# Reading expert sums later: a two-block network on one Trainium2 core, with a root table asked for elsewhere and thirty unread products at the start

## The chip, the core and the metric

The kernel runs on one core of a Trainium2 chip. The metric is device time in microseconds (us) of one execution; 2152.31 us is the median of three runs before the change. The engines that matter here are TensorE (PE; the loading of its stationary operand is PEld), VectorE (DVE), ScalarE (ACT) and the queue of SyncE (SP), which issues the transfers. GpSimd (POOL) does next to nothing.

## The reference, cut to what matters

A first block (adaptive norm, a mixer of three branches, a feed-forward layer) and two further layers run on 256 tokens of width 1024, all in float32. The last part is the mixture of experts, in which most of the bytes lie:

```python
cond = jax.nn.silu(c)
mod = (cond @ w_ada[l] + b_ada[l])[:, None, :]           # shift, scale and gate of the first norm
...
out = jnp.zeros_like(h)
for e in range(N_EXPERTS):                               # 8 experts, D 1024, inner width 3584
    out = out + gates[..., e:e+1] * ((jax.nn.silu(h @ wg[e]) * (h @ wu[e])) @ wd[e])
x = x + g2 * out
return rmsnorm(x, final_norm_w)                          # one last root for each token
```

## The kernel before, in words

**Products in three parts.** Each float32 weight is split into a high part (fp32r) and a low rest. `split` does it in two instructions on blocks of 128x1024: ACT copies the source to the high part (a CAST, L374), DVE subtracts that from the source for the low part (L339). `chunk` fetches a weight block of 1 MB (512x512) by one transfer into a raw buffer and splits it in two such splits; the raw buffer is free for the next transfer when both are through. `mm3` then makes three products of each pair (high by high, high by low, low by high). There are six pairs of split buffers in the expert stage.

**The expert stage.** The chosen tokens of an expert are gathered by products (`place`, `begin`, `gather`), go through seven blocks of 512 inner columns, and are added back by products (`scatter`). The four experts with most tokens are *large*, the others *small* (up to 64 tokens, whose high and low parts lie side by side in the stationary operand, so that two products do instead of three). Two chains of experts take turns, so that a step of a large expert is followed by one of a small one; such two steps are called a pair here. A step has 12 splits: four for `gate` (two chunks, `kh` 0 and 4), four for `up`, four for `down` of the step before (`prev`; two halves). Each product of 128x512 is one instruction on PE; a large step has 48 for gate and up and 24 for down, a small one 32 and 16.

**Who reads the sums.** ACT, DVE and PE work through their instructions in the order written. In `up`, the sum of gate is read by ACT straight behind gate's splits (L351, a Silu of 128x512, large; the small one's copy L2128 behind up's splits). `up_end`, behind the splits of down's first half, multiplies (DVE) or copies (ACT, L2138) the sum of up and turns the result by four transposes, or eight small products, on PE. `end`, in the next step behind gate's first chunk (`mids[0]`), copies the turned result as high part (ACT, L2160) and subtracts (DVE); down needs both. `mids` is a list of four places in the next step, behind each of its four chunks. `issue_after(i)` keeps an instruction behind `i` on its engine; beyond that a scheduler sets the order, and the order printed below is what it made.

**The start.** `ada_start` multiplies a column block of `w_ada` by `cond`: eight terms per block, of which DVE adds seven in `acc` (L343, L348) and PE takes the eighth (`wv(7)`) and the sum over `acc` as products with one column. `ada_end` adds the bias; only then can the norm be scaled, split and multiplied. `warm(n)` issues `n` products of 128x512 whose result nobody reads.

**The end.** Behind the last step comes a branch (`overflow`, not taken here, for an expert with more tokens than places), then the rest of `down`, the last `scatter`, the squares, the roots (L574, `rsqrt_s`) and the output. A function of ACT needs its table loaded (ACT_TABLE_LOAD); `self.dummy` receives a result that nobody reads, to have a table loaded early.

Of the kernel before, what the change touches and what calls it, by code (L numbers as in the profile page):

```python
# [8 lines left out]
F32 = mybir.dt.float32  # L9
# [203 lines left out]
class K:  # L213
# [440 lines left out]
    def ada_start(self, w, cond, p, cb):  # L654
        acc = self.take("ma")
        with self.scope():
            w0, w1 = self.raw(w, 0, 4, cb * 512, 512), self.raw(w, 512, 4, cb * 512, 512)
            wv = lambda k: w0[:, k] if k < 4 else w1[:, k - 4]
            self.ts(acc, wv(0), cond[:, 0:1])
            for k in range(1, 7):  # L660
                self.stt(acc, wv(k), cond[:, k : k + 1], acc, ALU.mult, ALU.add)
            for l, r in ((wv(7), cond[:, 7:8]), (acc, self.ones[:, :1])):
                for j in range(4):
                    self.last_mm = self.mm(p[:, cb * 4 + j : cb * 4 + j + 1], l[:, j * 128 : j * 128 + 128], r, cb < 2 and j == 0 and l is not acc, cb > 1 and j == 3 and l is acc, True)
        self.free(acc)
# [95 lines left out]
    def setup(self):  # L761
# [15 lines left out]
        nc.scalar.copy(self.one, self.ones[:, :1])  # L777
# [56 lines left out]
    def block1(self):  # L834
# [17 lines left out]
        with self.scope("d"):  # L852
# [12 lines left out]
            for half in range(2):  # L865
                with self.scope("s"):
                    p = self.psum()
                    self.ada_start(A["w_ada"][0], self.cond1, p, half)
                    if half:
                        product(1, 0)  # L870
                    self.ada_start(A["w_ada"][0], self.cond1, p, 2 + half)
# [1159 lines left out]
    def scatter(self, acc, PG, add, gain=None, part=(0, 1)):  # L2031
        with self.scope():
            for half in part:
                cs = slice(half * 512, half * 512 + 512)
                with self.scope():
# [4 lines left out]
                    else:  # L2040
                        y = self.med()
                        self.tt(y, acc[half], gain[:, cs], ALU.mult)
                        if half == 0:
                            self.act(self.dummy, y[:, :1], AF.Sqrt, bias=self.eps, scale=0.0)
# [9 lines left out]
    def moe(self, x, lg, rs):  # L2054
# [49 lines left out]

        def up(e, cb, mids):
            XH, XL = state[e][1][0], state[e][1][-1]
            g, ps = self.med(), []
            for nm in ("moe_w_gate_2", "moe_w_up_2"):
                p = self.take("pd")
                ps.append(p)  # L2110
                for kh in (0, 4):
                    with self.scope():
                        args = (W(nm, e), kh * 128, 4, cb * 512, 512)
                        c = self.chunk(*args)
# [9 lines left out]
                if not small[e] and nm == "moe_w_gate_2":  # L2124
                    self.act(g, p, AF.Silu)
            if small[e]:
                with self.tc.issue_after(self.last_hi.ins):
                    nc.scalar.copy(g, ps[0])  # L2128
            return g, p


        def up_end(e, g, pu):
            hu = self.take("r", 0)
            p = self.take("ps", 0)
            if small[e]:
                gu = self.med()
                with self.tc.issue_after(self.last_hi.ins):
                    nc.scalar.copy(gu, pu)  # L2138
                for i, a in enumerate((g, gu)):
                    for k in range(4):  # L2140
                        self.mm(p[:, i * 256 + k * 64 : i * 256 + k * 64 + 64], a[:, k * 128 : k * 128 + 128], self.cst("ident2"))

                def end():
                    with self.scope():
                        h = self.med()
                        self.act(h[:, :256], p[:, :256], AF.Silu)
                        self.tt(h[:, 256:], p[:, 256:], h[:, :256], ALU.mult)
                        v = hu[:, :512].rearrange("p (k h s) -> p k h s", k=4, h=2)
                        self.split(h[:, 256:].rearrange("p (k s) -> p k s", k=4), v[:, :, 0], v[:, :, 1])
                    self.free(p)  # L2150
                return hu, end
            with self.scope():
                h = self.med()
                self.tt(h, pu, g, ALU.mult)
                for k in range(4):
                    self.tr(p[:, k * 128 : k * 128 + 128], h[:, k * 128 : k * 128 + 128])

            def end():
                with self.tc.issue_after(self.last_hi.ins):
                    self.last_hi = nc.scalar.copy(hu[:, :512], p)  # L2160
                with self.tc.issue_after(self.last_lo.ins):
                    self.tt(hu[:, 512:], p, hu[:, :512].bitcast(F32), ALU.subtract)
                self.free(p)
            return hu, end

        def down(e, cb, hu, half):
            hh, hl = hu[:, :512], hu[:, 512:]
# [3 lines left out]
            with self.scope():  # L2171
                c = self.chunk(W("moe_w_down_2", e), cb * 512, 4, half * 512, 512)
                for k in range(4):
# [7 lines left out]
            if half:  # L2181
                self.free(hu)
# [19 lines left out]
        for e, cb in steps:  # L2202
            with self.scope():
                gp = up(e, cb, mids)
                mids = [[] for _ in range(4)]
                if cb == NB - 1:
                    self.free(*state[e][1])
                if prev:
                    down(*prev, 0)
                hu, end = up_end(e, *gp)  # L2210
                mids[0].append(end)
# [3 lines left out]
            prev = (e, cb, hu)  # L2215
# [25 lines left out]
        for half in range(2):  # L2241
            self.presplit(W("moe_w_down_2", NE - 1), (NB - 1) * 512, 4, half * 512, 512)
        self.q["pd"].append(self.q["ps"].popleft())
        self.overflow(x, gate, pos, scaled, ad, add, PP[0], cap)
        down(*prev, 0)
# [67 lines left out]
```

## Time and profile before

| | us |
|---|---|
| median of three runs | 2152.31 |
| the three runs | 2149.79, 2152.31, 2153.07 |
| the profiled execution | 2151.22 |
| its span, from first to last instruction | 2149.4 |

| engine | busy, share of the span |
|---|---|
| PE | 96% |
| DVE | 86% |
| ACT | 62% |
| PEld | 79% |

PE's share is an upper bound: its matmuls are pipelined and their ends modelled, so a matmul that waits behind its weights counts as busy. The waits for a semaphore are given by who waited and by which instruction ended the wait. Everything below is told in the profiled execution's own time (1.8 us of it lie outside the span), which is 1.1 us under the median.

### The profile page before, as it was taken

The page shows a single profiled execution, that of the slowest core. Times are in us where ns is not written, and L with a number is a line of the kernel's source. Part 1 is how long each engine was busy: PE and PEld are TensorE (multiplying, and loading weights), DVE is VectorE, ACT ScalarE, POOL GpSimd, SP SyncE. Part 2 cuts the span into 40 slices and gives each one's busy share as a digit, 9 for nine tenths or more (in the row PEclk, how much of TensorE's full clock was granted, in tenths as well). Part 3 has the DMA queues.
Part 4 walks back from the last instruction along what each step waited for, and adds up shares of the span by engine and source line. Part 5 has one row for each costly group of instructions (what it writes and reads, how often), then busy time and mean ns, then how long its engine had stood idle before and what let it go on. Part 6 is the DMA issues. An engine that isn't in the chain of part 4 may idle for free. (4 is left out here: it accounts for less than half of the span.)

```text
span 2149.4 us, 31135 instructions
## 1 busy us (share of the span) xinstructions
PE 2066.2 (96%) x11593; PEld 1706.1 (79%) x11593; DVE 1841.5 (86%) x2669; ACT 1325.3 (62%) x1857; POOL 2.1 (0%) x6
## 2 busy tenths in 40 slices
PE   6999999999999999999999999999999999999997
PEld 5987888889988878998997887777777777777765
DVE  6888985898888868888787999998998899998997
ACT  4544354454445435444765887777787778777775
POOL 0000000000000000000000000000000000000000
PEclk9999999999999999999999999999999999999997
DMA  7546767878843527885465899998999899998993
GB/s 306 192 165 214 264 219 255 298 296 303 302 160 117 150 100 262 310 342 212 139 253 188 329 400 368 356 387 321 391 343 377 348 365 377 355 383 322 386 371 140
DMA packets 99997, 610.70 MB, mean 284 GB/s; under 512 B 19156, under 2 KB 24061, under 8 KB 27773
## 3 DMA queue, kind: packets, MB, share of 16 engines
q1 hardware_dynamic: 99836, 608.64, 75.7%
q8 instruction: 92, 1.51, 0.3%
q14 instruction: 69, 0.56, 0.1%
HBM read 606.75 MB, written 3.42 MB: 284 GB/s over the span
## 5 line engine op out<-in xcount | busy, mean ns | idle before, releaser
L354 PE MATMUL pd<-k 128*128 128x512 f32 (+2 forms) x7408 | 1447.2, 349 | 37.8 <-DVE k L339 26.6
L339 DVE TENSOR_TENSOR k<-k,k 128x1024 fp32r<-128x1024 f32 (+2 forms) x1149 | 1229.8, 1112 | 184.4 <-ACT k L374 180.9
L354 PEld LDWEIGHTS pd<-k 128*128 128x128 f32 (+1 forms) x7408 | 1139.1, 190 | 269.3 <-DVE k L339 104.0
L374 ACT CAST k<-k 128x1024 fp32r<-128x1024 f32 (+2 forms) x1131 | 1039.6, 977 | 362.9 <-PE pd L354 184.6
L354 PE MATMUL ps<-k 128*128 128x512 f32 (+8 forms) x3031 | 576.2, 343 | 13.4 <-DVE k L339 3.8
L354 PEld LDWEIGHTS ps<-k 128*128 128x128 f32 (+4 forms) x3031 | 431.6, 179 | 112.1 <-DVE k L339 18.2
L348 DVE SCALAR_TENSOR_TENSOR k<-k,k 128x512 f32<-128x512 f32 (+1 forms) x257 | 188.3, 735 | 2.1 <-ACT k L351 0.2
L351 ACT ACTIVATE k<-pd 128x256 f32<-128x256 f32 (+1 forms) x125 | 57.2, 481 | 101.4 <-PE pd L354 98.5
L351 ACT ACTIVATE k<-k 128x256 f32<-128x256 f32 (+8 forms) x142 | 69.0, 500 | 79.3 <-DVE k L339 41.7
L339 DVE TENSOR_TENSOR k<-k 128x512 f32<-128x512 f32 (+13 forms) x277 | 93.6, 355 | 17.3 <-ACT k L351 12.4
L354 PEld LDWEIGHTS ps<-k,k 128*128 128x128 f32 x526 | 77.0, 199 | 12.4 <-DVE k L348 3.4
L339 DVE TENSOR_TENSOR k<-ps,k 128x512 fp32r<-128x512 f32 (+5 forms) x99 | 56.8, 579 | 24.8 <-PE ps L354 8.7
L354 PE MATMUL ps<-k,k 128*128 128x64 f32 (+3 forms) x526 | 75.0, 269 | 2.9 <-DVE k L348 2.9
L357 PE MATMUL ps<-k,k 128*128 128x128 f32 (+1 forms) x396 | 60.8, 278 | 16.7 <-DVE k L343 15.8
L357 PEld LDWEIGHTS ps<-k,k 128*128 128x128 f32 (+1 forms) x396 | 47.9, 143 | 30.5 <-DVE k L343 18.5
L339 DVE TENSOR_TENSOR k<-pd,k 128x512 f32<-128x512 f32 (+4 forms) x108 | 59.8, 568 | 12.5 <-PE pd L354 6.5
L351 ACT ACTIVATE k<-ps,k 128x128 f32<-128x128 f32 (+2 forms) x100 | 36.6, 446 | 42.8 <-DVE k L348 26.7
L348 DVE SCALAR_TENSOR_TENSOR k<-pd,k,k 128x255 f32<-128x255 f32 (+2 forms) x96 | 43.1, 474 | 4.4 <-ACT k L351 4.0
L2138 ACT COPY k<-pd 128x512 f32<-128x512 f32 x28 | 16.4, 586 | 48.2 <-PE pd L354 47.9
L345 DVE TENSOR_SCALAR k<-ps,k 128x128 f32<-128x128 f32 (+1 forms) x90 | 32.4, 405 | 10.5 <-PE ps L354 6.9
L348 DVE SCALAR_TENSOR_TENSOR k<-k 128x256 f32<-128x256 f32 (+7 forms) x121 | 36.9, 312 | 2.8 <-ACT k L351 1.1
L351 ACT ACTIVATE k<-ps 128x256 f32<-128x256 f32 (+2 forms) x30 | 12.4, 420 | 35.3 <-PE ps L354 35.3
(95 smaller groups left out, 416.1 us busy)
## 6 DMA issues: line engine op xcount, KB each, us to landing
k<-in_moe_w_up_dram SPq DMA_DIRECT2D x112, 1024.0 KB, 7.0
k<-in_moe_w_gate_dram SPq DMA_DIRECT2D x112, 1024.0 KB, 7.1
k<-in_moe_w_down_dram SPq DMA_DIRECT2D x112, 1024.0 KB, 7.2
k<-in_ada_w_dram SPq DMA_DIRECT2D x48, 1024.0 KB, 5.3
k<-in_w_in_dram SPq DMA_DIRECT2D x44, 1024.0 KB, 6.1
k<-in_w_ff_dram SPq DMA_DIRECT2D x32, 1024.0 KB, 6.0
k<-in_w_ada_dram SPq DMA_DIRECT2D x24, 1024.0 KB, 6.7
k<-in_cd_w_in_dram SPq DMA_DIRECT2D x14, 1024.0 KB, 4.9
```

Of the source, the lines that this page charges most:

```text
L339: return self.nc.vector.tensor_tensor(o, a, b, op=op)
L345: self.nc.vector.tensor_scalar(o, a, s1, s2, op0=op0, op1=op1)
L348: self.nc.vector.scalar_tensor_tensor(o, a, s, b, op0=op0, op1=op1)
L351: return self.nc.scalar.activation(o, a, f, **kw)
L354: return self.nc.tensor.matmul(o, l, r, start=start, stop=stop, skip_group_check=skip)
L357: return self.nc.tensor.transpose(o, i, self.ident[: i.shape[0], : i.shape[0]])
L374: self.last_hi = self.nc.scalar.copy(hi, src)
L2138: nc.scalar.copy(gu, pu)
```

## The change

Three edits. In the expert stage `up` no longer reads its sums: ACT's reading of gate (`gate_out`) comes behind the splits of down's first half, the reading of up (`up_out`) behind gate's first chunk of the next step, the turn behind the second chunk of the next step, and `end` behind the splits of down's first half of the next step, ahead of down's products. The sums and the turned result now take turns in three banks of `pd`. At the start, two terms of each of the first two column blocks go to PE instead of one, and 30 unread products are issued behind the instruction that makes their operand. At the end, the request for the last root's table moves from `scatter` (where it read a result of the experts) to a place behind the branch in the program, where it reads a constant.

```diff
-    def ada_start(self, w, cond, p, cb):
+    def ada_start(self, w, cond, p, cb, own):
...
-            for k in range(1, 7):
-                self.stt(acc, wv(k), cond[:, k : k + 1], acc, ALU.mult, ALU.add)
-            for l, r in ((wv(7), cond[:, 7:8]), (acc, self.ones[:, :1])):
+            for k in range(1, 8):
+                if k not in own:
+                    self.stt(acc, wv(k), cond[:, k : k + 1], acc, ALU.mult, ALU.add)
+            terms = [(wv(k), cond[:, k : k + 1]) for k in own] + [(acc, self.ones[:, :1])]
+            for i, (l, r) in enumerate(terms):
                 for j in range(4):
...
-        nc.scalar.copy(self.one, self.ones[:, :1])
+        one = nc.scalar.copy(self.one, self.ones[:, :1])
+
+        self.warm(30, one)
...
-                    self.ada_start(A["w_ada"][0], self.cond1, p, half)
+                    own = (7,) if half else (3, 7)
+                    self.ada_start(A["w_ada"][0], self.cond1, p, half, own)
...
                         self.tt(y, acc[half], gain[:, cs], ALU.mult)
-                        if half == 0:
-                            self.act(self.dummy, y[:, :1], AF.Sqrt, bias=self.eps, scale=0.0)
                         self.split(y, yh, yl)
...
-                if not small[e] and nm == "moe_w_gate_2":
-                    self.act(g, p, AF.Silu)
+            return ps
+
+        def gate_out(e, b):
+            b["g"] = self.take("ms", 0)
+            with self.tc.issue_after(self.last_hi.ins):
+                if small[e]:
+                    nc.scalar.copy(b["g"], b["ps"][0])
+                else:
+                    self.act(b["g"], b["ps"][0], AF.Silu)
+            self.free(b["ps"][0])
+
+        def up_out(e, b):
+            b["h"] = self.take("ms", 0)
             if small[e]:
                 with self.tc.issue_after(self.last_hi.ins):
-                    nc.scalar.copy(g, ps[0])
-            return g, p
+                    nc.scalar.copy(b["h"], b["ps"][1])
+            else:
+                with self.tc.issue_after(self.last_lo.ins):
+                    self.tt(b["h"], b["ps"][1], b["g"], ALU.mult)
+            self.free(b["ps"][1])
+
+        def turn(e, b):
+            p = b["p"] = self.take("pd", 0)
...
+        def end(e, b):
+            p, hu = b["p"], self.take("r", 0)
+            hi, lo = self.last_hi.ins, self.last_lo.ins
...
+                with self.tc.issue_after(hi):
                     self.last_hi = nc.scalar.copy(hu[:, :512], p)
-                with self.tc.issue_after(self.last_lo.ins):
+                with self.tc.issue_after(lo):
                     self.tt(hu[:, 512:], p, hu[:, :512].bitcast(F32), ALU.subtract)
...
-        def down(e, cb, hu, half):
+        def down(e, cb, b, half, after=()):
...
                 c = self.chunk(W("moe_w_down_2", e), cb * 512, 4, half * 512, 512)
+                for f in after:
+                    f()
+                hh, hl = b["hu"][:, :512], b["hu"][:, 512:]
...
-                gp = up(e, cb, mids)
...
-                if prev:
-                    down(*prev, 0)
-                hu, end = up_end(e, *gp)
-                mids[0].append(end)
+                b = {"ps": up(e, cb, mids)}
+            mids = [[] for _ in range(4)]
...
+            if prev:
+                down(*prev, 0, [lambda: end(prev[0], prev[2]), lambda: gate_out(e, b)])
+            else:
+                gate_out(e, b)
+            mids[0].append(lambda e=e, b=b: up_out(e, b))
+            mids[1].append(lambda e=e, b=b: turn(e, b))
...
         for half in range(2):
             self.presplit(W("moe_w_down_2", NE - 1), (NB - 1) * 512, 4, half * 512, 512)
+        end(prev[0], prev[2])
         self.q["pd"].append(self.q["ps"].popleft())
         self.overflow(x, gate, pos, scaled, ad, add, PP[0], cap)
+
+        self.act(self.dummy, self.eps, AF.Sqrt)
         down(*prev, 0)
```

ACT in the expert stage, before, from a small step's two readings to the next step's `end` of a large one (L2128 and L2138: gate and up of the small step; L351 of 128x256: its `end`; L351 of 128x512: gate of the large step; L2160: `end` of the large step; `k_63` and `k_64` are the two buffer areas, `pd` the sums):

```order
L2128 COPY k_63<-pd_68 128x512
L374 CAST k_64<-k_63 128x1024 x2
L2138 COPY k_63<-pd_69 128x512
L374 CAST k_64<-k_63 128x1024 x2
L351 ACTIVATE k_63<-pd_66 128x256
L374 CAST k_64<-k_63 128x1024 x2
L374 CAST k_64<-k_63 128x4x64
L374 CAST k_64<-k_63 128x1024 x4
L351 ACTIVATE k_63<-pd_67 128x512
L374 CAST k_64<-k_63 128x1024 x8
L2160 CAST k_64<-pd_66 128x512
```

The same stretch after (L2177: `end` of the large step; L2134 and L2144: gate and up of the small step):

```order
L2177 CAST k_64<-pd_68 128x512
L2134 COPY k_63<-pd_69 128x512
L374 CAST k_64<-k_63 128x1024 x4
L2144 COPY k_63<-pd_67 128x512
L374 CAST k_64<-k_63 128x1024 x8
L351 ACTIVATE k_63<-pd_69 128x256
L374 CAST k_64<-k_63 128x1024
L374 CAST k_64<-k_63 128x4x64
L351 ACTIVATE k_63<-pd_68 128x512
L374 CAST k_64<-k_63 128x1024 x11
```

The reading of a large gate moved from behind that gate's own four casts (the row x4) to behind the ten of gate, up and half of down; the reading of a small gate moved by two casts, that of a small up by four; `end` moved from behind the next gate's first two casts to behind ten.

PE in the expert stage, before: gate, up, first half of down, the turn of a large result (four transposes, L357), second half, gate and up of the next step:

```order
L354 MATMUL pd_67<-k_64 128x512 x24
L354 MATMUL pd_68<-k_64 128x512 x24
L354 MATMUL ps_70<-k_64 128x512 x8
L357 MATMUL ps_72<-k_65,k_63 128x128 x4
L354 MATMUL ps_71<-k_64 128x512 x8
L354 MATMUL pd_69<-k_64 128x512 x16
L354 MATMUL pd_67<-k_64 128x512 x13
```

After, from gate of a small step to up of the next large one (`pd_66` and `ps_72` are the large expert's two sums of down, `pd_68` x4 the turn of the large result, the rows of 128x64 that of the small one):

```order
L354 MATMUL pd_69<-k_64 128x512 x16
L357 MATMUL pd_68<-k_65,k_63 128x128 x4
L354 MATMUL pd_67<-k_64 128x512 x16
L354 MATMUL pd_66<-k_64 128x512 x2
L354 MATMUL pd_69<-k_65,k_63 128x64 x4
L354 MATMUL pd_66<-k_64 128x512 x10
L354 MATMUL ps_72<-k_64 128x512 x12
L354 MATMUL pd_68<-k_64 128x512 x24
L354 MATMUL pd_69<-k_65,k_63 128x64 x4
L354 MATMUL pd_67<-k_64 128x512 x24
```

The number of products is the same. The turn moved from between the halves of down to behind the next step's gate, and down now follows an `end` that stands two splits ahead of it.

ACT behind the branch, before (L351 of 128x1 is the request for the table, L351 x4 the squares, L574 the roots):

```order
L2260 UNCONDITIONAL_BRANCH x2
L351 ACT_TABLE_LOAD
L351 ACTIVATE k_65<-k_63,k_65 128x1
L374 CAST k_64<-k_63 128x512 x2
L351 ACTIVATE k_63,k_65<-k_63 128x512 x4
L574 ACTIVATE k_63<-k_63,k_65 128x1 x2
```

ACT behind the branch, after; and, as a piece of the difference, ACT far ahead of the expert stage, beside an older request of the same kind:

```order
L2285 UNCONDITIONAL_BRANCH x2
L374 CAST k_64<-k_63 128x512 x2
L351 ACTIVATE k_63,k_65<-k_63 128x512 x4
L574 ACT_TABLE_LOAD
L574 ACTIVATE k_63<-k_63,k_65 128x1 x2
```

```order
-L351 ACTIVATE k_65<-k_65 128x1
+L351 ACTIVATE k_65<-k_65 128x1 x2
```

The request, which now reads a constant alone, was moved by the scheduler out of the place where it is written to far ahead, where other tables are loaded behind it. The table of the roots is loaded behind the squares.

PE behind the branch, before (the first row is what is left of down) and after:

```order
L354 MATMUL ps_70<-k_64 128x512 x3
L354 MATMUL ps_71<-k_64 128x512
L354 MATMUL ps_73<-k_64 128x512
```

```order
L354 MATMUL ps_71<-k_64 128x512 x8
L354 MATMUL ps_70<-k_64 128x512 x8
L354 MATMUL ps_73<-k_64 128x512
L354 MATMUL pd_66<-k_64 128x512
```

All 16 products of the last down stand behind the branch now, before 3 did.

## Rows read from the trace of the kernel before

**Rows 1.** Windows by stage: us, busy time (and count) of each engine, clock, DMA.
```profile
0.00:60.00 60.00, 43.17 (x193) 36.36 (x194) 41.40 (x68) 26.91 (x45) 0.20 (x4) 0.97 0.77 300
60.00:1172.00 1112.00, 1089.21 (x7196) 957.71 (x7195) 922.77 (x1693) 544.98 (x891) 1.91 (x2) 0.99 0.63 226
1172.00:1254.40 82.40, 82.40 (x397) 68.91 (x396) 76.84 (x95) 69.02 (x81) 0.00 (x0) 1.00 0.86 320
1254.40:1284.10 29.70, 29.70 (x142) 24.64 (x142) 29.28 (x30) 23.97 (x29) 0.00 (x0) 1.00 1.00 408
1284.10:2046.90 762.80, 738.64 (x3334) 559.54 (x3333) 683.37 (x692) 590.05 (x723) 0.00 (x0) 1.00 0.94 363
2046.90:2130.60 83.70, 77.29 (x329) 55.73 (x327) 78.97 (x79) 64.48 (x78) 0.00 (x0) 0.96 0.76 293
2130.60:2149.40 18.80, 5.82 (x12) 3.15 (x11) 8.87 (x16) 5.91 (x14) 0.00 (x0) 0.55 0.16 58
```

**Rows 2.** Waits from 1284.1 to 2046.9: total us, times, longest us.
```profile
PEld pd L354 <- DVE k L339: 85.1, 181, 1.1
DVE k L339 <- ACT k L374: 66.7, 61, 6.7
ACT k L351 <- PE pd L354: 56.9, 28, 3.8
ACT k L2138 <- PE pd L354: 38.8, 20, 2.3
```

**Rows 3.** Waits of the transfer queue in the same stretch, the only row.
```profile
SPq L393 <- DVE k L339: 621.1, 263, 9.1
```

**Rows 4.** Groups by shape, same stretch: busy us, mean ns, idle before, releasers.
```profile
L339 DVE TENSOR_TENSOR k<-k,k 128x1024 fp32r<-128x1024 f32 x527 | 611.5, 1216 | 66.3 <-ACT k L374 66.0
...
L374 ACT CAST k<-k 128x1024 fp32r<-128x1024 f32 x527 | 516.0, 1052 | 0.9 <-PE pd L354 0.9
...
L351 ACT ACTIVATE k<-pd 128x512 f32<-128x512 f32 x23 | 13.8, 598 | 48.6 <-PE pd L354 48.6
```

**Rows 5.** Timeline inside two pairs: start, us, engine, instructions, idle before, releaser.
```profile
1606.10 0.59 ACT L2160 CAST k<-ps 128x512 fp32r<-128x512 f32 x1 [1.24 <-PE ps L357]
...
1609.62 0.68 DVE L339 TENSOR_TENSOR k<-ps,k 128x512 fp32r<-128x512 f32 x1
...
1618.41 0.59 ACT L2138 COPY k<-pd 128x512 f32<-128x512 f32 x1 [2.30 <-PE pd L354]
...
1622.22 3.01 PE L354 MATMUL ps<-k 128*128 128x512 f32 x12
...
1630.74 0.60 ACT L351 ACTIVATE k<-pd 128x512 f32<-128x512 f32 x1 [1.91 <-PE pd L354]
...
1632.30 4.63 DVE L339 TENSOR_TENSOR k<-k,k 128x1024 fp32r<-128x1024 f32 x4 [1.26 <-ACT k L374]
```

**Rows 6.** Timeline where one expert ends and the next is gathered.
```profile
1454.91 0.60 ACT L351 ACTIVATE k<-pd 128x512 f32<-128x512 f32 x1 [3.77 <-PE pd L354]
...
1460.08 5.23 DVE L339 TENSOR_TENSOR k<-k,k 128x1024 fp32r<-128x1024 f32 x5 [3.12 <-ACT k L374]
```

**Rows 7.** Timeline of the start, up to the first scaled norm.
```profile
12.62 1.11 PE L357 MATMUL ps<-k,k 128*128 128x128 f32 x4 [12.62 <-DVE k L343]
...
14.76 3.89 DVE L348 SCALAR_TENSOR_TENSOR k<-k,k 128x512 f32<-128x512 f32 x5
...
23.82 1.87 PE L354 MATMUL ps<-k,k 128*128 128x1 f32 x8 [1.55 <-DVE k L348]
...
25.56 4.50 PE L354 MATMUL ps<-k 128*128 128x512 f32 x10
```

**Rows 8.** Timeline behind the branch.
```profile
2134.11 1.62 PE L354 MATMUL ps<-k 128*128 128x512 f32 x3 [3.45 <-PEq L2260]
...
2134.86 1.28 ACT L351 ACT_TABLE_LOAD   x1 [6.17 <-DVE k L339]
...
2142.66 0.61 ACT L574 ACTIVATE k<-k,k 128x1 f32<-128x1 f32 x2
```

## What was predicted

> **What bounds the kernel now.** I read the busy time by stage first, then who waits for whom, then the timeline of single pairs. The stages before 1172 us are ordered by the change as before, but for the first 60 us; PE is busy for 1089 of 1112 us there [rows 1] and nothing in the diff reaches them. So the prediction is about three places: the expert stage (1172 to 2131 us), the first 30 us and the last 19 us.
>
> In the expert stage no engine is full. From 1284.1 to 2046.9 us lie 22 pairs of a large and a small step (23 readings of a large gate, one at each edge [rows 4]), 34.7 us each. DVE is busy for 683.4 of the 762.8 us, ACT for 590.1, the transfers for 0.94 of the time [rows 1]. DVE's idle 79.4 us end in 66.7 us on a cast of ACT [rows 2]. Is ACT too slow? Its cast takes 1052 ns against DVE's 1216 ns, and in front of its own casts ACT waits only 0.9 us in all [rows 4]. It is late because of what stands in its queue: 48.6 us before the 23 readings of a large gate [rows 4], 38.8 us before the copies of a small up, all ended by PE [rows 2]. One such place shows the mechanism: ACT stands still for 1.91 us until PE has finished gate, then needs 0.60 us to read it, and DVE has meanwhile run out of high parts for 1.26 us [rows 5]. ACT throws away the lead that it has over PE at every step, and PE then waits for DVE's low parts, 85.1 us in 181 small waits [rows 2]. No wait of ACT for a transfer is among the rows; the queue's transfers wait for DVE to free a raw buffer, 621 us [rows 3].
>
> That the three engines can go faster together is seen in one pair: from 1254.4 to 1284.1 us it took 29.7 us, with PE busy throughout, DVE for 29.28 us, and the transfers at 408 GB/s [rows 1].
>
> **Expert stage, the reading moved back.** The work is the same, instruction by instruction; only places change. A gate sum of a large step is now read behind ten casts of its step instead of four, the reading of up behind fourteen. There are six pairs of split buffers, so the cast that stands ahead of such a reading could not have started before PE had used the pair six splits earlier: by then the sum is finished, or nearly so. So ACT's waits for gate and up should go, and with them most of the 66.7 us of DVE.
>
> What is late next? DVE itself: 683.4 us of work. To this I add the 0.42 us that DVE was idle in the fast pair, 22 times: 9 us. The third part is the change of experts, six of them in the stretch, where ACT reads what the gather's products leave; that reading has no later place. At one of them DVE lacked a cast for 3.12 us, partly because ACT had waited 3.77 us for a gate sum [rows 6]. That part goes; I keep 4 us per change for the rest (gather, scatter), 24 us. 683.4 + 9 + 24 = 716 us, **46 us less** than 762.8. PE would allow it: 22 pairs at 29.7 us are 653 us, and at 0.25 us per product (12 in 3.01 us [rows 5]) the eight products of a scatter, and about as much again or a little more for a gather, make some 5 us per change, 685 us in all (an estimate). Bounds: if only the 48.6 us of large gates counted and a third of it reached DVE, 16 us; if DVE ran as in the fast pair and the changes cost nothing, 70 us.
>
> Before 1254 us PE is busy in every microsecond [rows 1], so nothing is won there. In the last small steps (2046.9 to 2130.6 us) DVE is busy for 78.97 of 83.7 us; I take 2 of the 4.7 idle us.
>
> **The new wait.** Down's products now need an `end` that is queued behind both splits of that half: two splits at 1.16 us (four in 4.63 us), a copy of 0.59 us, of which the subtraction of 0.68 us waits [rows 5]: 3.6 us at most from the moment when PE could have begun. Behind it on PE stand all of down, the next gate and the turn; DVE and ACT go on. It is covered where PE is behind DVE by more than that. A step with a large up and small down gives PE 64 products of 0.24 to 0.25 us and a turn, about 16.5 us, against 12 splits of DVE and the small `end`, about 14.7 us, so PE falls behind and arrives late. In the other kind of step PE has 56 products, about 14 us, against 15.2 us, and catches up by about 1.2 us less than it fell behind. So I cost the wait at nothing; it is the first rival below. The narrow turn behind two products of down needs ACT's copy of gate, queued straight behind `end`: 0.2 us at most, inside the wait for the subtraction.
>
> On SP the loads of the experts' numbers now stand together ahead of one transfer more. They wait for the ranking at about 1175 us, when the transfers are busy for 0.86 of the time [rows 1]; the stock of raw buffers hides a few us. Zero.
>
> **The start.** DVE saves one term in each of two blocks: 5 terms in 3.89 us, 0.78 us each, 1.56 us on the chain that ends with the four products of `acc` (recorded as eight) at 23.82 us, for which PE had waited [rows 7]. PE gains two groups of four products, each 1.87 us at the rate of that row, in gaps that were open before: from 14.9 to 23.8 us its other groups took about 5.3 us, so 3.7 more just about fit. The thirty products run while PE waits for its first work at 12.62 us [rows 7]. Ten such products took 4.50 us (0.45 us each, the lower of the clock's two levels, 1.2 GHz, though the column shows no drop there) [rows 7], 12 in 3.01 us at the upper [rows 5]; thirty from 2.2 us on end at about 15.7 us if all run at the lower level and at about 9.7 us at the upper one. If the clock is high when the groups run, each takes about half, and the chain ends up to 2.5 us earlier; if it is low, PE is the end of the chain and it is up to 2 us later. I take **1 us less**; PE is full after it, so it reaches the end.
>
> **The end.** The request for the table does not stay where it is written: the order puts it far ahead, and a load of 1.28 us now stands between the squares and the first root. So 1.28 us plus the request's 0.3 us leave the chain at 2134.86 us, and 1.28 us come back before 2142.66 us [rows 8]: 0.3 us won, not 1.6. Against that, 16 products stand behind the branch where 3 did; these took 1.62 us, 0.54 us each, at a clock of about half [rows 8]. They need only the last low part of `end`, so some run during the 3.45 us in which the engines go through the branch [rows 8]. 13 more at 0.45 to 0.54 us are 6 to 7 us; less the 3.45 us, about 3 us. The last `end` stands bare: one more hop between ACT and DVE, about 0.5 us. Together **3 us more** (bounds: 4 less if the clock holds, 6 more if nothing overlaps).
>
> **Sum.** 2151.2 - 46 - 2 - 1 + 3 = 2105 us, in the profiled execution's time, 1.1 us under the median shown.
>
> **The rivals.** (1) *PE runs dry at down.* If the 3.6 us wait is bare in every step, a pair costs 29.7 + 7.2 = 36.9 us instead of 34.7, 48 us more over 22 pairs: 2151 + 48 + 2, about 2200 us. It turns the sign once the bare part is over 2.5 us per step on average (half of 34.7 - 29.7). For it: the two splits and the copy are strictly ahead. Against: DVE and ACT keep working ahead during the wait, and PE's large step is longer than DVE's. Chance 0.08.
>
> (2) *The transfers are the bound.* At 716 us the stretch needs 363 x 762.8 / 716 = 387 GB/s, with the transfers already busy for 0.94 of the time. If 363 GB/s were what can be had over long stretches, DVE's idle time would only change its name: 2150 us. The fast pair ran at 408 GB/s, and no wait for a transfer shows, so chance 0.05. The Trainium skill has a rule to this effect (DMA: Bandwidth & Descriptors, "Where 436 GB/s comes from"): between HBM and on-chip memory some 358 GB/s per core bind, and by it the stage would gain nothing. The trace disagrees: 363 GB/s over 763 us and 408 GB/s in a pair are above it; the same page's measured 425 GB/s for one core alone fits better.
>
> (3) *The waits come back.* DVE runs ahead and then waits for split buffers that PE holds, or the changes of experts spread their stall over the neighbouring pairs. The idle time before PE's weights is 85.1 us in many small waits [rows 2], some of which are DVE's own pace. A third of the gain would stay: 2151 - 16 + 2, about 2136 us. Chance 0.15.
>
> **How the numbers follow.** Forecast 0.72, (3) 0.15, (1) 0.08, (2) 0.05. The forecast's own range is 2078 to 2126 us (70 us won to 25 us won in the stage, with the ends of start and end). With most of (3) the range is 2078 to 2140 us; left out are (1), (2), a part of (3) and a corner below. Faster by over 0.2% (4.3 us, about what can be told from no change): 0.72 + 0.15 = 0.87; the same 0.05; slower 0.08.
>
> **What the profile after would show.** Right: readings of gate and up with hardly any idle time before them; DVE's wait for casts from 66.7 us to under 30; pairs of 30 to 33 us; transfers near 390 GB/s; a table load ahead of the first root. Wrong: PE waiting for ACT's copy of `end` before down by 2 us or more per step (1); ACT waiting for transfers (2); ACT or DVE waiting for PE's release of split buffers, with pairs still over 33.5 us (3).

## The result

| | us |
|---|---|
| kernel before, median on the same chip | 2151.05 |
| changed kernel, median | 2118.32 (2117.22 to 2124.44) |
| ratio, with 95% interval | 0.9854 [0.9832, 0.9876] |
| profiled execution of the changed kernel, and its span | 2124.44, 2121.5 |

The change wins 32.7 us, where 46 were forecast. The profiled execution is the slowest of the four. Part of that lies where the change does nothing: the exponential of the router, the last step ahead of the experts, began at 1164.6 us here, and between 1157.6 and 1164.6 us in all nine kernels that have the changed start. So I compare stretches, not spans, and measure the expert stage from that exponential to the end of DVE's last low part ahead of the branch ("the stage"), and the rest from there ("the end"). The stage repeats well from kernel to kernel: 969.3 and 969.0 us in the two kernels with the old expert part, 934.3 to 935.4 us in the six with the new one.

| us | before | changed | difference |
|---|---|---|---|
| up to the router's exponential | 1161.3 | 1164.6 | +3.3 |
| the stage | 969.25 | 935.37 | -33.9 |
| in it: 22 pairs between 23 readings of a large gate | 762.8 | 730.2 | -32.6 |
| the end | 18.86 | 21.58 | +2.7 |

### The profile page after: what moved, and what is told of

It is laid out like the page before. It is cut to its first block, busy times and chain, and to the rows that moved or that the text cites. A ratio compares the mean times of both kernels' runs of the same rounds, so it can differ in the third digit from the quotient of the medians.

```text
span 2121.5 us, 31382 instructions
## 1 busy us (share of the span) xinstructions
PE 2043.6 (96%) x11639; PEld 1740.5 (82%) x11639; DVE 1841.2 (87%) x2667; ACT 1336.6 (63%) x1857; POOL 2.1 (0%) x6
## 5 line engine op out<-in xcount | busy, mean ns | idle before, releaser
L354 PE MATMUL pd<-k 128*128 128x512 f32 (+2 forms) x7414 | 1416.4, 347 | 23.3 <-DVE k L339 14.3
L354 PE MATMUL ps<-k 128*128 128x512 f32 (+5 forms) x3055 | 573.2, 345 | 28.6 <-DVE k L339 17.5
L354 PEld LDWEIGHTS ps<-k 128*128 128x128 f32 (+2 forms) x3055 | 449.0, 182 | 125.2 <-DVE k L339 27.6
L351 ACT ACTIVATE k<-k 128x256 f32<-128x256 f32 (+9 forms) x143 | 69.2, 498 | 79.5 <-DVE k L339 42.2
L351 ACT ACTIVATE k<-pd 128x256 f32<-128x256 f32 (+1 forms) x148 | 65.7, 463 | 47.4 <-PE pd L354 44.6
L354 PE MATMUL pd<-k,k 128*128 128x64 f32 (+1 forms) x472 | 69.8, 288 | 5.8 <-ACT k L2134 5.1
L354 PEld LDWEIGHTS pd<-k,k 128*128 128x128 f32 x472 | 63.6, 193 | 12.1 <-ACT k L2134 6.2
L351 ACT ACTIVATE k<-ps,k 128x128 f32<-128x128 f32 (+2 forms) x100 | 37.3, 447 | 34.2 <-DVE k L348 27.1
L357 PE MATMUL ps<-k,k 128*128 128x128 f32 x302 | 47.2, 281 | 5.2 <-DVE k L343 4.3
L339 DVE TENSOR_TENSOR k<-ps,k 128x512 f32<-128x512 f32 (+5 forms) x52 | 30.8, 605 | 23.1 <-PE ps L354 15.0
L357 PEld LDWEIGHTS ps<-k,k 128*128 128x128 f32 x302 | 36.7, 145 | 15.5 <-DVE k L343 7.1
L345 DVE TENSOR_SCALAR k<-ps,k 128x128 f32<-128x128 f32 (+1 forms) x90 | 32.7, 405 | 12.2 <-PE ps L354 8.8
L357 PE MATMUL pd<-k,k 128*128 128x128 f32 (+1 forms) x222 | 36.8, 281 | 4.0 <-DVE k L1351 4.0
L357 PEld LDWEIGHTS pd<-k,k 128*128 128x128 f32 (+1 forms) x222 | 28.1, 143 | 10.9 <-DVE k L1351 4.4
```

The costliest lines, as they stand in the source:

```text
L339: return self.nc.vector.tensor_tensor(o, a, b, op=op)
L345: self.nc.vector.tensor_scalar(o, a, s1, s2, op0=op0, op1=op1)
L351: return self.nc.scalar.activation(o, a, f, **kw)
L354: return self.nc.tensor.matmul(o, l, r, start=start, stop=stop, skip_group_check=skip)
L357: return self.nc.tensor.transpose(o, i, self.ident[: i.shape[0], : i.shape[0]])
```

## The profile after

Windows of the changed kernel, columns as in [rows 1]: the first full pair and the 22 pairs behind it.

```profile
1260.20:1290.38 30.18, 30.18 (x144) 25.24 (x143) 29.94 (x31) 26.55 (x32) 0.00 (x0) 1.00 1.01 410
1290.38:2020.58 730.20, 704.68 (x3332) 576.97 (x3331) 684.52 (x694) 600.68 (x725) 0.00 (x0) 0.99 0.97 380
```

DVE's work in the 22 pairs is what it was, 684.5 us; its idle time fell from 79.4 to 45.7 us. ACT's groups by shape in that stretch:

```profile
L374 ACT CAST k<-k 128x1024 fp32r<-128x1024 f32 x528 | 526.6, 1051 | 66.6 <-PE pd L354 46.4 <-PE ps L354 14.5 <-issue 2.6
L351 ACT ACTIVATE k<-pd 128x512 f32<-128x512 f32 x23 | 13.6, 591 | 0.0
L2144 ACT COPY k<-pd 128x512 f32<-128x512 f32 x22 | 12.9, 588 | 0.0
L2134 ACT COPY k<-pd 128x512 f32<-128x512 f32 x22 | 12.9, 585 | 0.0
```

No reading of gate or up is waited for any more (48.6 us before the large gates alone [rows 4]); DVE's 22 multiplications of a large up have no idle time before them either. ACT now stands ahead of its casts instead, 66.6 us where it was 0.9 [rows 4]: it is as far ahead as the six pairs of split buffers let it, and PE's release of a buffer ends the wait. The waits of the same stretch (total us, times, longest us) say who still suffers:

```profile
ACT k L374 <- PE pd L354: 48.5, 110, 2.1
DVE k L339 <- ACT k L374: 33.4, 47, 4.5
...
PE ps L354 <- DVE k L339: 16.1, 16, 2.4
ACT k L2003 <- PE ps L357: 14.0, 5, 5.8
```

DVE's wait for casts fell from 66.7 [rows 2] to 33.4 us. Where its largest pieces lie, the timeline shows. L2003 is the copy by which `place` reads its turned slots; PE is still in the products of a large step when ACT comes to it.

```profile
1518.99 3.25 PE L354 MATMUL pd<-k 128*128 128x512 f32 x13
...
1522.49 0.38 ACT L2003 CAST k<-pd 128x256 fp32r<-128x256 f32 x1 [5.77 <-PE pd L357]
...
1523.85 2.36 DVE L339 TENSOR_TENSOR k<-k,k 128x1024 fp32r<-128x1024 f32 x2 [4.53 <-ACT k L374]
```

This is the mechanism that the change removes, at a place which the change leaves as it was: ACT waits 5.77 us in front of a sum that PE reaches late, and DVE is out of casts for 4.53 us. ACT waits for 1.0 to 5.8 us at the other five such copies, too (the row of 14.0 us), and behind all six DVE is out of casts for 13.6 us together.

## The experiments

**One edit at a time.** The expert edit alone on the kernel before, and the start alone.

```diff
 # the expert edit alone: the changed kernel with
-        self.warm(30, one)
-                    own = (7,) if half else (3, 7)      # ada_start as before
-        self.act(self.dummy, self.eps, AF.Sqrt)         # the request back in scatter
```

> The edit of the expert stage alone on the kernel before; start and request for the table as before. My terms of the prediction, corrected by the trace after: 23 pairs of 33.06 instead of 34.45 us give 32 us, the last steps and the bare end cost about 2, so 2151 - 30 = 2121 us; a pair 33.1 us. By the prediction as written (start 1 us won, the request at the end 0.3 us won): the whole change's 2118 us plus 1, 2119 us. If the start after costs 1 us, as its trace suggests, this kernel is 1 us faster than the whole change: 2117 us. In the trace: the first product behind the start's norm at 49.4 us as before.

0.9842 [0.9829, 0.9855]; the stage 934.3 us, the end 17.6 us. The whole gain is the expert edit's, and alone it has an end that is 4 us shorter than in company.

```diff
 # the start alone: the kernel before with
+        self.warm(30, one)
+                    own = (7,) if half else (3, 7)
```

> The start alone on the kernel before (thirty products and the terms given to PE). Prediction: 1 us won, 2150 us; the products behind the start's norm begin a microsecond earlier than 49.35 us. Rival, from the trace after: PE's clock has fallen when the groups of one-column products run, PE is now the end of that chain, and the clock falls once more at 38 us: 1 us lost, 2152 us, the product at 50.3 us. Second rival: the microsecond in the trace after was a later arrival of the transfers (0.55 us at the first term), and nothing is won or lost.

0.9996 [0.9987, 1.0005], nothing that the time can tell. The product behind the norm came at 49.34 us as before (49.35), but PE's first work on data had come 0.75 us later (13.37 for 12.62 [rows 7]). From there to the ten unread products it is 12.16 us instead of 12.94, and to the product behind the norm 35.97 instead of 36.73, so 0.8 us are won on the chain. The second rival (arrival) holds for the rest: PE's first work came as late, at 13.28 and 13.22 us, in two kernels with the start of before.

**The thirty products.** The changed kernel without them.

```diff
-        self.warm(30, one)
```

> The changed kernel without its thirty unread products; two terms per block still go to PE. Theory A (the thirty products make the clock fall at 14 us, and PE's way through the branch longer): the clock holds while the one-column products run, the ten unread products come 11 us after PE's first work instead of 12.15, and the end takes 19 us as with the start of before. Theory B (the terms do it): clock 0.5 from 15 us on, 12.2 us, and 21.5 us at the end. The time is 0 to 3 us under that of the whole change.

0.9851 [0.9836, 0.9866], as the whole change. At the start theory A falls: 12.15 us with and without the thirty. The changed kernel: its last group of one-column products in the timeline, then the window from 14 to 28 us (the clock is the third figure from the end).

```profile
18.48 6.98 PE L354 MATMUL ps<-k,k 128*128 128x1 f32 x32 [0.41 <-DVE k L348]
```

```profile
14.00:28.00 14.00, 12.75 (x56) 12.07 (x56) 10.00 (x19) 2.03 (x5) 0.00 (x0) 0.52 1.02 424
```

The same two views of the kernel without the thirty:

```profile
18.08 6.99 PE L354 MATMUL ps<-k,k 128*128 128x1 f32 x32 [0.23 <-DVE k L348]
24.93 4.61 PE L354 MATMUL ps<-k 128*128 128x512 f32 x10
```

```profile
14.00:28.00 14.00, 13.77 (x58) 13.10 (x59) 9.83 (x18) 2.43 (x6) 0.00 (x0) 1.00 1.01 423
```

The clock's column differs (0.52 and 1.00), the 32 products take 6.98 and 6.99 us. The 0.8 us come from DVE's saved terms. The thirty products buy nothing: behind them eight one-column products took 0.95 us at 13.67 us, but behind a gap of PE of 0.84 us the next eight, at 16.37 us, took 1.71 us, as without the thirty (1.71 us at 16.14). At the end the number is A's, 19.0 us; whether the thirty are its cause is taken up below.

**The end.** The request back in the scatter, the start as before, and the request behind the first cast of the last scatter.

```diff
 # request as before                                     # start as before: see the first diff
+                        if half == 0:
+                            self.act(self.dummy, y[:, :1], AF.Sqrt, bias=self.eps, scale=0.0)
-        self.act(self.dummy, self.eps, AF.Sqrt)
```

> The changed kernel with the request for the roots' table back in the scatter, as before. The kernel with the expert edit alone ended 17.6 us after DVE's last instruction before the branch, the changed one 21.6 us after it; this run and the next tell which of the two other edits costs these 4 us. Theory A, the moved request does: 17.6 us here and about 4 us less time than the whole change (2113 us). Theory B, the start does (its 38 more instructions on PE stand ahead of the branch): 21 us or more here, the time as that of the whole change or 0.3 us above. Theory C, it is chance of one execution: anything from 17 to 22 us here and in the next.

> The changed kernel with the start as before. Theory A (the moved request costs the 4 us at the end): 21.6 us from DVE's last instruction before the branch to the end, the time as that of the whole change. Theory B (the start does): 17 to 18 us, some 4 us less time. At the start itself: the ten unread products 12.94 us after PE's first work instead of 12.15.

```diff
 # request behind the first cast, in scatter
                         self.split(y, yh, yl)
+                        if half == 0:
+                            with self.tc.issue_after(self.last_hi.ins):
+                                self.act(self.dummy, self.eps, AF.Sqrt)
...
-        self.act(self.dummy, self.eps, AF.Sqrt)
```

> The changed kernel, with the request for the roots' table put behind the first cast of the last scatter. Theory: in the changed kernel the load of 1.28 us lies bare between the squares and the first root; here it lies between two casts that wait for PE anyway: the stretch from DVE's last instruction before the branch to the end from 21.6 to 20.3 us, the time 1.3 us less than the whole change (2117 us). Rival: the load only pushes the second cast, whose sum DVE reads at once, and nothing is won: 21.6 us.

0.9843 [0.9829, 0.9856], 0.9839 [0.9825, 0.9852] and 0.985 [0.9836, 0.9863]: in time none differs from the whole change. The traces do:

| start | request | PE idle in the branch, us | the products behind it | the end, us |
|---|---|---|---|---|
| as before | as before (expert edit alone) | 2.61 | 16 in 3.96 | 17.6 |
| as before | moved | 2.61 | 16 in 3.94 | 19.1 |
| changed | as before | 4.27 | 16 in 5.53 | 19.6 |
| changed | moved (the change) | 4.13 | 17 in 6.70 | 21.6 |
| changed | behind the first cast | 4.09 | 16 in 5.96 | 20.8 |
| no thirty | moved | 2.60 | 16 in 3.92 | 19.0 |

In these rows, one execution each, the moved request costs 1.5 us (first two) or 1.9 us (next two). The expert edit alone, behind the branch (DVE, ACT):

```profile
2094.78 3.96 PE L354 MATMUL ps<-k 128*128 128x512 f32 x16 [2.61 <-DVE k L339]
2097.99 0.69 DVE L339 TENSOR_TENSOR k<-ps,k 128x512 f32<-128x512 f32 x1 [3.26 <-DVEq L2282]
2098.76 1.28 ACT L351 ACT_TABLE_LOAD   x1 [4.49 <-DVE k L339]
2098.84 0.69 DVE L339 TENSOR_TENSOR k<-ps,k 128x512 f32<-128x512 f32 x1 [0.15 <-PE ps L354]
```

and the one with the start as before and the request moved:

```profile
2099.21 3.94 PE L354 MATMUL ps<-k 128*128 128x512 f32 x16 [2.61 <-DVE k L339]
...
2102.69 0.69 DVE L339 TENSOR_TENSOR k<-ps,k 128x512 f32<-128x512 f32 x1 [3.54 <-DVEq L2281]
2104.12 0.69 DVE L339 TENSOR_TENSOR k<-k,k 128x512 fp32r<-128x512 f32 x1 [0.74 <-ACT k L374]
2104.73 0.68 DVE L339 TENSOR_TENSOR k<-ps,k 128x512 f32<-128x512 f32 x1
...
2110.24 1.28 ACT L574 ACT_TABLE_LOAD   x1
```

With the request in scatter, DVE reads both sums of down one behind the other, the second while ACT loads the table (2097.99, 2098.84). Without it, DVE's low part of the first half stands ahead of the reading of the second (2102.69, 2104.12, 2104.73), and the load comes bare at the end. So the load and request of before were not simply 1.6 us on the chain: DVE's second reading ran beside them. That is read from these rows; no run changes the order of the two readings alone. Behind the first cast the request won 0.8 of the 1.3 us expected, with one more load of 1.28 us ahead of that cast.

The other 2.1 to 2.5 us go with PE's longer way through the branch and the low clock that follows (6.70 us for 17 products at a granted clock of 0.59, instead of 3.96 for 16 at 1.00). The thirty products go with the long way in all six rows, but a kernel below that has them took 2.61 us, and one without them ran its 17 products in 7.24 us, at 0.57, behind 2.62 us. What decides both is left open. Nor is theory C, chance of one execution, out: four kernels below with the start and the request of the change end in 19.3 to 21.4 us.

**What is left at the changes of experts.** `place`'s copy read two chunks later, in the next step:

```diff
-            p = self.psum()
+            p = self.take("ps", 0) if later is not None else self.psum()
...
-            self.nc.scalar.copy(PG, p[:, :256])
+            def read():
+                with self.tc.issue_after(self.last_hi.ins) if later is not None else nullcontext():
+                    self.nc.scalar.copy(PG, p[:, :256])
...
+            read() if later is None else later.append(read)
...
+            mids[0] += later
+            later.clear()
```

> The changed kernel, with ACT's copy of place's turned slots (L2003) read two chunks of casts later, in the next step. Theory A (what is left at the changes of experts is ACT standing before that copy; DVE lacks casts behind its six places for 1.1 to 4.6 us, 13.6 us in all): 10 to 13 us less than the whole change, 2106 us, and the pairs with a place 1 to 4.5 us shorter. Theory B (those pairs are full for PE, whose products of gather and scatter come on top, and DVE's idle time there is slack): only PE's own idle behind it comes back, 1.3 us at two places: 2115 to 2118 us, while L2003 no longer waits.

0.9841 [0.9828, 0.9855]; 2115.0 us in all, which is still within B; the stage took 929.9 us instead of 935.4, between the theories: 5 us of 13. L2003 no longer waits, but the wait has moved to ACT's readings of gather's sums (L351), and DVE starves there. Waits in its 22 pairs, then two rows of its timeline:

```profile
DVE k L339 <- ACT k L374: 31.7, 37, 3.9
...
ACT k L351 <- PE ps L354: 21.2, 5, 5.0
```

```profile
1668.94 0.70 ACT L351 ACTIVATE k<-ps,k 128x64 f32<-128x64 f32 x2 [4.99 <-PE ps L354]
...
1670.61 2.36 DVE L339 TENSOR_TENSOR k<-k,k 128x1024 fp32r<-128x1024 f32 x2 [3.94 <-ACT k L374]
```

So gather's sums were read one chunk later as well, on the same scheme:

```diff
-            return [lambda k0=k0: self.gather(x, P, ad["a2"], ad["b2"], out, (k0,)) for k0 in (0, 4)]
+            go = lambda k0: self.gather(x, P, ad["a2"], ad["b2"], out, (k0,), later)
+            return [lambda: go(0), lambda: (later.pop(0)(), go(4)), lambda: later.pop(0)()]
...
-                return [lambda: self.gather_small(x, P, ad["a2"], ad["b2"], X)]
+                return [lambda: self.gather_small(x, P, ad["a2"], ad["b2"], X, later), lambda: later.pop(0)()]
```

> As the kernel with place's copy read later, and the sums of gather are read one chunk later too. In that kernel the wait had moved: its pairs of 42.3 and 35.9 us hold ACT's readings of gather's sums, which wait for PE for up to 5.0 us (21.2 us in all), and DVE lacks casts for 3.6 to 3.9 us behind them. Theory A (ACT standing before sums at the changes of experts is what is left): DVE's wait for casts from 31 to under 15 us, 8 to 12 us less time than that kernel, 2104 us. Theory B (PE and DVE are full there in turn): the wait goes on to the next place, at most 3 us less.

0.9755 [0.9742, 0.9769], 2098.2 us: **20 us less than the change**, and the fastest of all. The stage took 915.9 us. Its 22 pairs and its waits:

```profile
1283.46:1994.29 710.83, 695.24 (x3331) 574.70 (x3330) 682.51 (x694) 603.88 (x725) 0.00 (x0) 1.00 0.97 390
```

```profile
DVE k L339 <- ACT k L374: 17.3, 39, 2.1
```

Theory A in sign, and more than it in size: 16.7 us less than the kernel before it (14.0 in the stage) where 8 to 12 were named, though DVE's wait for casts fell to 17.3 us and not to under 15. PE is busy for 695.2 of the 710.8 us (an upper bound), DVE for 682.5. The seven pairs from one change to the next (us, the same seven in each kernel) show the wait travel:

| kernel | | | | | | | | sum |
|---|---|---|---|---|---|---|---|---|
| before | 32.4 | 32.4 | 36.1 | 35.1 | 33.6 | 34.2 | 39.9 | 243.7 |
| changed | 34.7 | 33.3 | 38.5 | 29.2 | 33.5 | 31.2 | 33.6 | 233.9 |
| and place later | 30.0 | 29.8 | 42.3 | 29.2 | 29.9 | 35.9 | 33.5 | 230.6 |
| and gather later | 30.1 | 29.8 | 41.3 | 29.1 | 30.0 | 34.6 | 33.4 | 228.2 |

These seven gained least from gather's move, 2.4 of the 14.1 us by which the 22 pairs became shorter. The six ahead of them gained 7.1 us and the seven behind 4.6, most of it in the pair that answers to the third of these, from 44.7 and 42.3 to 39.7 us each. The pairs with a change of experts stay at 33 to 41 us; what fills them now was not taken apart.

**And scatter later?** It begins one chunk later, too; then the same with start and request as before the change.

```diff
-                for i, f in zip((1, 2), down(*prev, 1) or []):
+                for i, f in zip((2, 3), down(*prev, 1) or []):
```

> As the kernel with place's and gather's sums read later, and scatter too begins one chunk later. There ACT's cast of down's sum for scatter still waits 2.7 us for PE and DVE lacks casts for 17 us in all. Theory A: these 17 us of DVE fall to under 10, 3 to 6 us less than that kernel (2098 us): 2093 us. Theory B (PE and DVE are full in turn): within 2 us of it.

> The same, with the start and the request for the roots' table as before the change. If the two edits cost at the end what the four kernels with each of them on and off show (17.6 us with neither, 21.6 us with both), and the start gives back 0.8 us: 3 us less than the kernel without this. If they cost nothing: 0 to 1 us more than it.

0.979 [0.9777, 0.9804] and 0.9785 [0.9771, 0.9798]: 7 us slower than without this edit, the stage 923.0 and 923.5 us. Neither theory said so. Here DVE reads scatter's products just behind their issue, ahead of the small `end` for which PE waits:

```profile
1580.09 0.75 DVE L348 SCALAR_TENSOR_TENSOR k<-pd,k 128x512 f32<-128x512 f32 x1 [2.15 <-PE pd L354]
...
1588.11 5.44 PE L354 MATMUL ps<-k 128*128 128x512 f32 x16 [2.04 <-DVE k L339]
```

In the kernel without this edit the two waits are 1.50 and 1.27 us, and the pair in which the second lies takes 29.1 us, here 30.7. These rows fit, but no run splits the 7 us further: the cause stays open. Start and request made no difference of 3 us: the ends took 19.3 us in both.

**The new wait.** `end` ahead of the two splits of down's first half instead of behind them:

```diff
-                down(*prev, 0, [lambda: end(prev[0], prev[2]), lambda: gate_out(e, b)])
+                down(*prev, 0, [lambda: gate_out(e, b)])
+            mids[3].append(lambda e=e, b=b: end(e, b))
...
-        end(prev[0], prev[2])
```

> The changed kernel with the turned result read (`end`) behind the fourth chunk of the next step, ahead of the two splits of down's first half instead of behind them; that takes away the new wait. In the changed kernel PE and its weights wait for DVE ahead of products into down's sums (`ps`) for 39 us in 41 waits between 1290 and 2021 us. Theory A (the wait, costed at nothing in the prediction, is bare): PE gets 16 us or more back, pairs 0.7 us shorter. Theory B (it was covered; those waits are DVE's pace): the time within 3 us of the whole change, DVE as busy as before.

0.9888 [0.9872, 0.9903], 7 to 8 us slower than the change; both theories fall. Waits in its 22 pairs:

```profile
PEld pd L354 <- DVE k L339: 50.9, 102, 1.5
DVE k L339 <- ACT k L374: 46.0, 44, 3.5
...
ACT k L351 <- PE pd L354: 19.1, 9, 3.9
...
PE ps L354 <- DVE k L339: 6.3, 13, 0.5
```

PE's waits at down do shrink (6.3 us where it was 16.1), but ACT and DVE lose their lead again: PE's weights wait for DVE for 50.9 us (21.7 in the changed kernel), DVE for casts for 46.0 (33.4). The late `end` is on balance part of the gain, not a price.

**Is DVE the bound now?** One more DVE instruction of 128x512 per step, read by nobody:

```diff
+        J = self.take("ma", 0)
...
+            with self.tc.issue_after(self.last_lo.ins):
+                self.tt(J, J, J, ALU.mult)
```

> The changed kernel with one more DVE instruction of 128x512 per step, about 0.7 us, which nobody reads, 1.4 us per pair. Theory A (DVE is the bound in the quiet pairs, and in the pairs with a place, gather or scatter PE or ACT's waiting is): pairs of 29.2 to 31.2 and of 33.6 us get 1.4 us longer, those of 33.3, 33.5 and 34.7 us stay: about 4 of 7, 18 us more. Theory B (DVE bounds everywhere): 32 us more over 23 pairs. Theory C (PE bounds everywhere, DVE has 4 us per pair in reserve): under 8 us more.

0.991 [0.9896, 0.9923]. The added group, and the 22 pairs:

```profile
L339 DVE TENSOR_TENSOR k<-k 128x512 f32<-128x512 f32 x44 | 30.3, 688 | 0.0
```

```profile
1291.09:2032.61 741.52, 713.19 (x3333) 573.98 (x3332) 708.71 (x739) 600.62 (x725) 0.00 (x0) 0.99 0.96 374
```

30.3 us of work lengthen the pairs by 11.3 us (741.5 - 730.2), 0.5 of 1.4 us per pair, between theories A and C. The pairs part only in part as A said: the seven grew by 0.6, 0.6, 0.6, 1.2, -0.5, 0.6 and 1.1 us. The last two of the 22, with no change of experts in them, grew from 29.7 and 29.8 to 30.8 and 30.9 us, by 1.0 to 1.1 of the 1.4 us added, so there DVE is close to the bound. In most others it has a reserve; it is not the one bound of the changed stage.

## Why the prediction was right, and where not

**Right: the mechanism and the sign.** Readings of gate and up have no idle time before them, and the gain is the expert edit's alone (0.9842). Two of the signs came out just outside of what was named: pairs of 33.1 us on average (23 from 1260.2 to 2020.6 us; 30 to 33 named), and DVE's wait for casts at 33.4 us (under 30 named).

**Mis-sized: the changes of experts.** The pairs were forecast 14 us too short, and this is the term. The sum for 22 pairs was 683.4 + 9 + 24 = 716 us; it came to 730.2. DVE's work was right (684.5). The idle time was 45.7 us instead of 33; if the 9 us of the quiet pairs hold, 36.7 us fall on six changes, 6.1 us each instead of 4. The step that failed is "that reading has no later place". It has one: with place and gather read later the 22 pairs took 710.8 us, with 28.3 us of idle time, under the 716 that I forecast for the change. I had looked at one change of experts [rows 6], where a gate's wait and a gather's stood together, and not at the copy of `place`: before the change it waited 8.0 us (five waits of 5.9 in all and one of 2.1) in the same stretch, as I read it because ACT had lost its time earlier; now 19.8 us (14.0 and one of 5.8), with DVE out of casts for 13.6 us behind it.

**Half right: what is late next.** "DVE itself" holds for a third of added work. PE's release of buffers holds ACT, a sign of rival 3, but the pairs of 33.1 us stay under the 33.5 that it named; no run takes its price apart from that of the changes of experts.

**Right as far as it is shown: the new wait at nothing.** Rival 1 is out, with 2118 us where it gave 2200. The wait is not absent: PE waits ahead of down for 16.1 us in 16 places. The edit that takes most of it away costs 7 to 8 us elsewhere, so what the 16.1 us cost by themselves is not shown.

**Right: the transfers do not bind.** 380 GB/s in the pairs, 410 in the first, 390 with the later readings; their queue still waits for DVE's release of raw buffers (585.4 us in the 22 pairs, 621.1 before [rows 3]). The rule of the Trainium skill weighed in rival 2 (DMA: Bandwidth & Descriptors, "Where 436 GB/s comes from", some 358 GB/s) would have kept the time at 2150 us; the measured rates disagree with it for one core alone.

**The start: right in size, for one of its two reasons.** DVE is done 1.5 us earlier after PE's first work (9.64 us instead of 11.15), as forecast from the two saved terms; 0.8 us of it are left on the chain, since PE then ends it, as the bound said. The thirty products change nothing.

**The end: right in sum (3, measured 2.7) by luck, wrong in both terms.** The 16 products behind the branch cost nothing by themselves: with the expert edit alone the end is 17.6 us, 1.3 less than before, the case "if the clock holds" (16 in 3.96 us). The request was put at 0.3 us won and costs 1.5 to 1.9 in the rows above; the load is off the casts' way, as forecast, but the order of DVE's two readings changed with it. The rest, 2.1 to 2.5 us, is PE's way through the branch and the clock behind it, which I had not as a term.

## What to carry to other kernels

When readings are moved back in one place of a loop, follow the same engine to the next reading that stands in front of its other work: the wait travels there, and a first move gains little until the next such readings are moved too (here 5 us for place alone, 14 more with gather; gather alone was not run). Move reads behind work that is ready, but measure each step: one chunk more for scatter gave back 7 of the 20 us, perhaps because its reads then came ahead of what PE waited for. A request for a table that reads a constant goes where the scheduler likes; look at the order, and at what ran beside the load before it is called a cost.

## What was not expected of the hardware

- The clock's column and the products' own times do not go together in the first 30 us: 32 one-column products took 6.98 us at 0.52 and 6.99 us at 1.00, and ten of 128x512 4.61 us at 1.00, against 2.43 us, also at 1.00 (45 us into the same kernel). I took the level from the durations there, not from the column; no run here decides between the two.
- PE's idle time in the same branch was 2.6 us in some kernels and 4.0 to 4.3 us in others (3.5 and 3.1 us in the two with the old expert part).
- The same instructions up to the router took between 1157.6 and 1164.6 us, 7 us from one kernel's execution to another's, a fifth of the gain.
- The table load took 1.28 us, and the root began 0.01 us behind it (2113.51 and 2114.80 us). The Trainium skill (ScalarE: Activation LUTs, "What ACT_TABLE_LOAD costs") adds a drain of some 1.38 us to each such load; no row here shows one.
